# A hybrid attention and SwiGLU layer: own places for each attention unit's stages, four-block products at the end, an opening in pieces over two queues

## The chip, the cores and the metric

One core of a Trainium2 chip runs the whole layer. The metric is device time in microseconds, the median of the runs shown. A run of this kernel varies by some 0.1%.

## The reference

A decoder layer on x (1 x 1024 x 1024, float32). Cut to what matters:

```python
h = rms_norm(x, ln_pre_mix)
proj = h @ w_in                       # pool 256, q 768, k 768, v 768
q, k = rope(q, pos), rope(k, pos)
pool_out = multi_scale_pool(u_pool, w_pool, pool_scale)
attn_out = dilated_attention(q, k, v) # 12 heads of 64; (window, dilation) (128,1) (512,4) (2048,16)
mix = concat([pool_out, attn_out]) @ w_out
x = x + rms_norm(mix, ln_post_mix)
h = rms_norm(x, ln_pre_ffn)
f = (silu(h @ w_gate) * (h @ w_up)) @ w_down
x = x + rms_norm(f, ln_post_ffn)
```

The three attention branches are merged per position and head by their softmax denominators.

## The kernel before, in words

Everything is kept transposed, features on the partitions and the 1024 positions along the free axis, in two halves h of 512. Every float32 operand is split into a high part (a rounded copy, made on ACT) and a low part (the rest, made on DVE or POOL), and a product is three passes on the tensor engine (PE): high x high, high x low, low x high (PASSES). PE's products are issued in program order (`mm`). On the other engines Tile's scheduler orders the instructions by priority, except for those given to `keep_in_program_order`, which keep their order among themselves.

*The opening* (lines 196 to 283). x comes in 8 tiles of 128 x 1024 (512 KB) through `load_x` (L234), the weights of the first head pair, w0[0] for q and w0[1] for k, in columns 0 to 2 and 2 to 8 of their 8 blocks through `load_w` (L226), all on SP's queue. Per x tile ACT makes the high part with g1 as its scale (L239), DVE the low part (L240), ACT a square (L246), DVE the running sum of squares (L248). `first(i, k)` (L220) has the 12 products of 512 columns of tile k for i: 6 for q, 6 for k. Ten products on zeros run ahead of it. The first value weights wv0 are split behind it (L273, with L154 and L158); products for v follow.

*The attention* (lines 304 to 880) has 12 units, one per head pair and half. A unit's stages are: scores (8 steps; PE, then the masked minimum on DVE, L554, and the exponential on ACT, L557), merge (`join`, L567: it exchanges row values through PE with ex, L577, and computes the weights wv in small DVE operations, L583 to L597), weigh (16 steps that scale the probabilities, on DVE, L611, or POOL, L613, by the table 'wd'), turn (transposes on PE, L653, split by ACT, L658, and DVE, L659) and products with v (L685), whose sums pass through L693, L694 and `into` (L623 to L627). Between them stand fill products: the projections of later pairs, of v and of the pool, in lists of 24 or so steps. At the end of a projection half `rope` (L331) runs: shuffle (L320) and cosine product (L321) on DVE, sine product (L322) and sum (L325) by the tables 'rq' and 'rk' on DVE (1) or POOL (0). 'we' says who makes the low part of a weight tile (1: DVE).

The order is a plan written by numbers: `put(steps, lo, hi)` lays a list of steps evenly between two places on an axis on which unit u starts at u, and `emit` (L782) issues all steps sorted by place. The table PRM holds the places: s0 and s1 for the scores, m for the merge, w0 and w1 for weigh, t0 and t1 for the turns, v0 and v1 for the products, one set for units of half 0 ('h0'), one for half 1 ('h1'). Besides, a planner clock runs along with assumed costs: where a step's due time has not come (`await_`, L368; 'lm' for the merge, 'lt' for a turn, 'ls' for a score bank), up to 'fl' fill products are pulled ahead.

*The rest.* The output projection, gate and up products and the down product follow, the latter as seven products of half-size blocks (P1 to P7). P3 is the last; it is cut into columns 0 to 256 and 256 to 512, each with an End (L1371): squares (L1390) and their sum as each row block is ready, the mean on PE (L1404), a power on POOL (L183), a transposition that spreads it (L1412), then `add(d)` for the 8 row blocks: a product with g4 and the spread value on DVE (L1418), the sum with x on DVE or POOL (L1422), and a transfer out (L1426) on SP's or ACT's queue.

Of the kernel before, what the change touches and what calls it, by code (L numbers as in the profile page):

```python
# [15 lines left out]
P = 128  # L16
T = 1024
# [13 lines left out]
        'sqa': (1, 0, 0, 1, 0, 0, 0, 1),  # L31
        'we': (1, 1, 1, 0, 0, 0, 0, 0, 0, 0, 1, 1),
        'nt0': 0.505,
        'nt1': 0.51,
        'oq': (0, 1, 1, 1, 0, 0, 0, 1),
        'lag': 3.0,
        'hp': 150,
        'fl': 12,
        'lt': 3.0,
        'ls': 2.2,  # L40
        'lm': 2.8,
        'lw': (3.5, 0.5),
        'nm': 0.02,
        'n2': -0.07638,
        'n0': 0.14,
        'n1': 0.3,
        'h0': {'s0': 0.0436,
               's1': 0.42346,
               'm': 0.62035,
               'w0': 0.76,  # L50
               'w1': 1.1342,
               't0': 0.85648,
               't1': 1.84986,
               'v0': 1.2506,
               'v1': 1.99965},
        'h1': {'s0': 0.0,
               's1': 0.55,
               'm': 0.63061,
               'w0': 0.76,
               'w1': 1.3742,  # L60
               't0': 0.96118,
               't1': 1.84958,
               'v0': 1.09322,
               'v1': 1.95471,
               'u0': 0.13504,
               'u1': -0.04663,
               'u2': 0.2974,
               'u3': 0.5838},
        'f0': -0.00645,
        'f1': 0.0,  # L70
        'first': {'s0': 0.48, 's1': 0.62, 'm': 0.7, 'w0': 0.78, 'w1': 1.06, 't0': 1.1},

        'vt': ((1.06, 1.08), (2.97, 3.3), (4.97, 5.3), (6.97, 7.3), (8.97, 10.27), (9.83, 10.29)),
        'pw': 0.5,
        'pm': (0.92, (0.78, 0, 0), (0.84, 1, 0), (0.99, 0, 1), (1.05, 1, 1)),
        'last': {'w1': 1.28, 't1': 1.62, 'v1': 1.74},
        'rq': (0, 0),
        'rk': (0, 0),
        'r0': (1, 1),
        'r1': (1, 1),  # L80
        'r2': (1, 1),
        'r3': (1, 1),
        'wd': (0, 1, 1, 0, 0, 0, 0, 0, 0, 0, 1, 0, 0, 0, 0, 0),
        'lr': (10.14, 10.15, 10.26, 10.27),
        'lw0': (10.1, 10.3),
        'lc': (11.63, 11.64, 11.66, 12.1),
        'o0': 10.36,
        'o1': 11.12,
        'o2': 12.85,
        'np': 11.62,  # L90
        'z0': 11.7,
        'z1': 13.05,
        'c0': (0.13, 0.2, 0.21, 0.6, 0.3, 0.7, 0.97, 0.09),
        'c1': (0.16, 0.25, 0.26, 0.84, 0.46, 0.97, 1.57, 1.7),
        'c2': ((0.95, 1.35), (1.4, 1.6)),
        'e0': ((0.26, 0), (0.42, 0), (0.47, 0.9)),
        'e1': (((1.08, 0), (1.28, 0), (1.3, 1.9)), ((2.0, 0), (2.01, 0), (2.02, 2.03)))}
# [10 lines left out]
def hybrid_block(ctx: ExitStack, tc: tile.TileContext, xT, w_in, w_v, w_pin, w_pool, w_out, w_gate, w_up, w_down,  # L108
# [44 lines left out]
    def split(dst, src, eng):  # L153
        nc.scalar.activation(dst[:, 0], src, AF.Copy)  # L154
        n = src.shape[-1]
        w = n if eng is nc.vector else n // 2
        for at in range(0, n, w):
            eng.tensor_tensor(dst[:, 1, at:at + w], src[:, at:at + w], dst[:, 0, at:at + w].bitcast(F32), ALU.subtract)  # L158
# [37 lines left out]
    g1s = cload(g1, [P, NK], "g1s", con1)  # L196

# [6 lines left out]
    nc.scalar.activation(small.tile([P, 1], F32, name="none", tag="none", bufs=1), ones, AF.Copy)  # L204
# [3 lines left out]
    for i in range(10):  # L208
        mm(wb, warm[:, :P], warm, start=True, stop=True)
# [10 lines left out]
    def first(i, k):  # L220
        for a, b in PASSES:
            for h in range(2):
# [3 lines left out]
    def load_w(i, lo, hi):  # L226

        sl = slice(lo * P, hi * P)
        nc.sync.dma_start(w0r[i][:, sl].rearrange("p (k m) -> p k m", m=P), w_in[i][:, lo:hi])
        split(w0[i][:, :, sl], w0r[i][:, sl], nc.vector)  # L230
# [3 lines left out]
    def load_x(k, lo=0, hi=T):  # L234
        if lo == 0:
            xr0.append(att.tile([P, T], F32, name="xraw", tag="pp", bufs=PPB))
        r, sl = xr0[k], slice(lo, hi)
        nc.sync.dma_start(r[:, sl], xT[:, k, sl])
        nc.scalar.activation(xk[k][:, 0, sl], r[:, sl], AF.Copy, scale=g1s[:, k:k + 1])  # L239
        nc.vector.scalar_tensor_tensor(xk[k][:, 1, sl], r[:, sl], g1s[:, k:k + 1], xk[k][:, 0, sl].bitcast(F32),  # L240
                                       op0=ALU.mult, op1=ALU.subtract)

    def square(k):
        r = xr0[k]
        d = att.tile([P, T], F32, name="jk", tag="ptr", bufs=PTB) if k else sq
        nc.scalar.activation(d, r, AF.Square)  # L246
        if k:
            nc.vector.tensor_tensor(sq, sq, d, ALU.add)  # L248

    load_x(0, 0, 512)  # L250
    load_w(0, 0, 2)
    load_x(0, 512, T)
    load_w(1, 0, 2)
    for i in range(2):
        first(i, 0)
    load_x(1)
    for i in range(2):
        load_w(i, 2, NK)
    for i in range(2):
        first(i, 1)  # L260
    for k in range(2, NK):
        load_x(k)
        square(k - 2)
        if k < NK - 2:
            for i in range(2):
                first(i, k)
# [36 lines left out]

    def pinned(x):
        return tc.keep_in_program_order(x)
# [404 lines left out]
    def pool_weights():  # L710
        for n in range(2):
            pool.w[n] = wtile(w_pin[n], nc.vector)

    def pool_proj(tt, k, n):

        if k == n == 0 and tt % 2 == 0:
            pool.ps = bank("t" if tt % 4 else "pj")
        ps = pool.ps[:, (tt % 2) * 256:(tt % 2) * 256 + 256]
        a, b = PASSES[n]
        mm(ps, xk[k][:, b, tt * P:(tt + 1) * P], pool.w[k // 4][:, a, (k % 4) * 256:(k % 4) * 256 + 256],  # L720
           start=(k + n == 0), stop=(k == NK - 1 and n == 2))
        if k == NK - 1 and n == 2 and tt % 2:
            h = tt // 4
            if tt % 4 == 1:
# [7 lines left out]
            due["u", h] = clock[0] + 3.2  # L732

# [7 lines left out]
    def pool_means(i, h):  # L741

        did(("means", i, h))
        await_(("u", h))
# [128 lines left out]
    fill[10] += [vl[12:]]  # L873
    for u in range(1, 11):
        put(Fill([x for f in fill[u] for x in f]).by(3), u + (G["f0"] if u > 1 else -0.07), u + (0.25 if u == 10 else 1) + G["f1"])
# [3 lines left out]
    put([pool_bands], G["pw"], 0)  # L879
# [491 lines left out]
    class End:  # L1371


        def __init__(self, h):
            self.h, self.jk, self.x, self.n = h, {}, [], 0

        def load(self):
            for n in range(2):
                x = place(("b4", "b5")[n], [P, 4, 512], F32, "xe")
                nc.sync.dma_start(x, x1d[4 * n:4 * n + 4, :, self.h * 512:self.h * 512 + 512].rearrange("k p t -> p k t"))  # L1380
                self.x += [x[:, i] for i in range(4)]

        def add(self, d, lo, hi, last):
# [4 lines left out]
            else:  # L1388
                jk = strip("p", 2)[:, :hi - lo]
                nc.scalar.activation(jk, src, AF.Square)  # L1390
                if last:
                    self.jk[lo] = jk
                else:
                    nc.vector.tensor_tensor(self.sq[:, lo:hi], self.sq[:, lo:hi], jk, ALU.add)
            self.n += 1

        def finish(self, lo, hi, tags):
# [17 lines left out]
            def add(d):  # L1415
                yd = yrow(self.h, d)[:, lo:hi]
                at_end = self.h and hi == 512
                i = nc.vector.scalar_tensor_tensor(yd, yd, g4s[:, d:d + 1], box["rb"], op0=ALU.mult, op1=ALU.mult)  # L1418
                eng = nc.gpsimd if at_end and d in (0, 2, 4) else nc.vector
                if at_end:  # L1420
                    tc.keep_in_program_order(i)
                i = eng.tensor_tensor(yd, yd, self.x[d][:, lo:hi], ALU.add)  # L1422
                if at_end and eng is nc.vector:
                    tc.keep_in_program_order(i)
                at = self.h * 512
                (nc.scalar if hi == 512 and self.h and G["oq"][d] else nc.sync).dma_start(  # L1426
                    out[d * P:(d + 1) * P, at + lo:at + hi], yd)
            return [mean], [rows], [lambda d=d: add(d) for d in range(NK)]
# [142 lines left out]
```

## Time and profile before

| | |
|---|---|
| median of 3 runs | 1167.78 us (1166.33 to 1168.17) |
| the profiled execution's own time | 1168.91 us |
| its span (first to last instruction) | 1167.1 us |
| mean granted PE clock | 0.990 |
| PE, DVE, POOL, ACT busy | 97%, 68%, 52%, 47% |
| instructions | 17255 |
| moved by DMA | 188.51 MB |

The profile is one execution. A stage is judged by what PE waits for in it, since PE carries the work: the groups, the waits and the windows are read for the stage, and not for the whole span.

### The profile page before, as it was taken

Reading aid. Unit: us, or ns where it says so; the run is one execution under the profiler, and the core shown is the slowest. Engines: PE = TensorE matmul, PEld = TensorE weight load, DVE = VectorE, ACT = ScalarE, POOL = GpSimd, SP = SyncE. Lnnn points to the kernel's source line nnn. Section 1 sums busy time; section 2 is a strip of 40 time slices with the busy share of each in tenths; the row PEclk is TensorE's granted clock in tenths of the full one; section 3 lists DMA queues with packets and bytes.
Section 4 is the critical chain, followed back from the end, with each engine's and each line's share of the span. In section 5 each row is a group of like instructions: output and inputs, shape, how many; then the busy total and the mean of one; then the engine's idle time right before and its main releaser. Section 6 shows DMA issues by size and latency. Waiting matters only on the chain.

```text
span 1167.1 us, 17255 instructions
## 1 busy us (share of the span) xinstructions
PE 1136.1 (97%) x6134; PEld 980.1 (84%) x6134; DVE 791.6 (68%) x1477; ACT 543.1 (47%) x1033; POOL 608.9 (52%) x541
## 2 busy tenths in 40 slices
PE   8999999999998999999999999999999999999996
PEld 6998889989888888888888888888888888888896
DVE  7766778787887675779686665766565465454685
ACT  7356667666566575656433222232232435343420
POOL 0111546565555403160586667777675978656521
PEclk9999999999999999999999999999999999999998
DMA  7315151415124744732233545444535789666542
GB/s 271 102 60 181 37 181 37 159 59 181 55 73 152 281 162 145 280 118 99 87 143 145 185 155 206 163 171 174 188 139 190 266 292 322 207 210 191 178 144 72
DMA packets 85365, 188.51 MB, mean 162 GB/s; under 512 B 8736, under 2 KB 24352, under 8 KB 83872
## 3 DMA queue, kind: packets, MB, share of 16 engines
q1 hardware_dynamic: 84704, 186.90, 46.2%
q8 instruction: 48, 0.79, 0.3%
q10 hardware_dynamic: 576, 0.52, 0.1%
q14 instruction: 37, 0.30, 0.1%
HBM read 134.44 MB, written 52.95 MB: 161 GB/s over the span
## 4 chain that ended last, share of the span: by engine, by line
PE 80%; DVE 8%; ACT 4%; DMA 3%; issue 3%; POOL 1%; SPq 0%; ACTq 0%; POOLq 0%; DVEq 0%
PE ps_pj L113 28%; PE ps_o L113 22%; PE ps_s L113 20%; PE ps_t L113 8%; PE ps_t L116 2%; ACT pp L557 1%; DMA mixd<-mix 1%; DVE z L1041 1%; DVE z L1040 1%; DMA m<-mixd 1%; DMA b<-in_w_out_dram 1%; DVE k L345 1%; DVE whl L158 1%; ACT whl L154 1%; DMA xraw<-in_xT_dram 1%
## 5 line engine op out<-in xcount | busy, mean ns | idle before, releaser
L113 PE MATMUL ps_pj<-x,whl 128*128 128x512 f32 x480 | 145.9, 418 | 0.0
L1225 POOL TENSOR_TENSOR fw<-rw,fw 128x512 fp32r<-128x512 f32 x74 | 102.6, 1414 | 62.9 <-ACT fw L1223 62.9
L613 POOL TENSOR_SCALAR pp<-pp,wv 128x256 f32<-128x256 f32 (+1 forms) x156 | 72.0, 480 | 104.9 <-DVE wv L597 52.1
L113 PE MATMUL ps_o<-tT,fw 128*128 128x512 f32 x504 | 118.1, 390 | 0.0
L158 POOL TENSOR_TENSOR whl<-wraw,whl 128x512 fp32r<-128x512 f32 x50 | 66.5, 1350 | 90.4 <-ACT whl L154 61.0
L113 PEld LDWEIGHTS ps_o<-tT,fw 128*128 128x128 f32 x504 | 94.6, 188 | 20.3
L557 ACT ACTIVATE pp<-pp,sx 128x128 f32<-128x128 f32 (+1 forms) x192 | 89.3, 468 | 30.0 <-DVE sx L554 29.4
L113 PEld LDWEIGHTS ps_pj<-x,whl 128*128 128x128 f32 x480 | 87.4, 194 | 10.3 <-POOL whl L158 0.4
L1225 POOL TENSOR_TENSOR whl<-rw,whl 128x512 fp32r<-128x512 f32 x42 | 62.5, 1511 | 58.0 <-ACT whl L1223 58.0
L1223 ACT ACTIVATE fw<-rw 128x1024 fp32r<-128x1024 f32 x37 | 38.5, 1058 | 100.7 <-DVE rw L1191 42.4
L113 PE MATMUL ps_pj<-whl,x 128*128 128x256 f32 x528 | 80.3, 293 | 0.0
L1367 POOL TENSOR_TENSOR op<-rw,op 128x512 fp32r<-128x512 f32 x38 | 60.6, 1594 | 35.5 <-ACT op L1366 34.2
L659 DVE TENSOR_TENSOR ptr<-ps_t,ptr 128x512 fp32r<-128x512 f32 (+1 forms) x84 | 56.2, 669 | 26.4 <-ACT ptr L658 25.8
L113 PEld LDWEIGHTS ps_pj<-whl,x 128*128 128x128 f32 x528 | 70.7, 196 | 0.5 <-DVE whl L158 0.2
L322 POOL TENSOR_TENSOR rsw<-rsw,sinr 128x512 f32<-128x512 f32 x20 | 26.2, 1309 | 84.7 <-DVE rsw L320 84.7
L658 ACT ACTIVATE ptr<-ps_t 128x512 fp32r<-128x512 f32 (+1 forms) x84 | 48.4, 576 | 40.6 <-PE ps_t L116 39.4
L1366 ACT ACTIVATE op<-rw 128x1024 fp32r<-128x1024 f32 x38 | 40.2, 1060 | 56.3 <-PE ps_t L113 32.2
L113 PE MATMUL ps_o<-ptr,v 128*128 128x128 f32 (+1 forms) x472 | 58.6, 258 | 4.8 <-DVE ptr L659 4.8
L113 PE MATMUL ps_pj<-b,fw 128*128 128x512 f32 x264 | 62.3, 392 | 0.0
L113 PEld LDWEIGHTS ps_o<-ptr,v 128*128 128x128 f32 x472 | 52.6, 164 | 8.8 <-DVE ptr L659 5.9
L113 PEld LDWEIGHTS ps_pj<-b,fw 128*128 128x128 f32 x264 | 49.6, 188 | 10.9
L113 PE MATMUL ps_s<-k,qh 128*128 128x128 f32 (+1 forms) x192 | 53.6, 291 | 0.3 <-DVE sx L554 0.2
(302 smaller groups left out, 2914.9 us busy)
## 6 DMA issues: line engine op xcount, KB each, us to landing
rw<-bd SPq DMA_DIRECT2D x77, 256.0 KB, 4.5
v<-vd SPq DMA_DIRECT2D x22, 512.0 KB, 4.9
rw<-wsd SPq DMA_DIRECT2D x44, 256.0 KB, 4.0
rw<-in_w_gate_dram SPq DMA_DIRECT2D x20, 512.0 KB, 3.6
rw<-in_w_up_dram SPq DMA_DIRECT2D x20, 512.0 KB, 4.5
bd<-p SPq DMA_DIRECT2D x33, 256.0 KB, 2.9
rw<-in_w_down_dram SPq DMA_DIRECT2D x33, 256.0 KB, 4.4
fw<-in_w_down_dram SPq DMA_DIRECT2D x16, 512.0 KB, 4.1
```

The costliest lines, as they stand in the source:

```text
L113: return tc.keep_in_program_order(nc.tensor.matmul(*a, **k))
L116: return tc.keep_in_program_order(nc.tensor.transpose(dst, src, by))
L158: eng.tensor_tensor(dst[:, 1, at:at + w], src[:, at:at + w], dst[:, 0, at:at + w].bitcast(F32), ALU.subtract)
L322: eng[0].tensor_tensor(s, s, sinr[:, sl], ALU.mult)
L557: nc.scalar.activation(pt[:, j, lo:], pt[:, j, lo:], AF.Exp, bias=sx[:, 0, side, j, hd, 0:1], scale=-1.0, accum_out=sx[:, 0, side, j, hd, ...
L613: nc.gpsimd.tensor_scalar(pv, pv, un.wv[:, side, j, hd:hd + 1], 1.0, op0=ALU.mult, op1=ALU.mult)
L658: nc.scalar.activation(ptr[:, 0, :w], t[:, :w], AF.Copy)
L659: nc.vector.tensor_tensor(ptr[:, 1, :w], t[:, :w], ptr[:, 0, :w].bitcast(F32), ALU.subtract)
L1223: nc.scalar.activation(w[n][:, :, 0], raw[n], AF.Copy)
L1225: low[0] = nc.gpsimd.tensor_tensor(w[n][:, i, 1], raw[n][:, i], w[n][:, i, 0].bitcast(F32), ALU.subtract)
L1366: nc.scalar.activation(w[:, :, 0], raw, AF.Copy)
L1367: nc.gpsimd.tensor_tensor(w[:, 0, 1], raw[:, 0], w[:, 0, 0].bitcast(F32), ALU.subtract)
```

## The change

It has three parts.

1. *Places.* PRM gets other values nearly throughout, and a new table 'du' with offsets of up to 0.08 for the places of single units. Some of the values: 'lm' 2.8 to 3.081, 'lt' 3.0 to 2.819, 'ls' 2.2 to 2.382, 'fl' 12 to 15; 'rk' (0, 0) to (1, 0): the sine product of each K rope goes from POOL to DVE; 'r0' (1, 1) to (0, 1): one sine product of the opening goes to POOL; 'wd' gets a fourth 1 among 16; 'we' from (1,1,1,0,0,0,0,0,0,0,1,1) to (0,0,0,0,0,1,0,0,0,1,1,1); 'pm', the places of the pool means, from (0.84, 1, 0), (0.99, 0, 1), (1.05, 1, 1) to (0.857, 1, 0), (1.025, 0, 1), (1.05, 1, 1), with their products 0.06 behind each. 'cut' is empty and 'pb' is 0, so `dealt` and the place of the bands change nothing.
2. *Opening.* `load_x` and `load_w` become fetch and split; all of them are pinned in program order. g1 and the first weight columns are issued on ACT's queue; x tiles 0 and 1 come and are split in halves of 512 columns, the weights in columns 0 to 2, 2 to 4 and 4 to 8; the squares move behind the splits; the last x tile has a buffer of its own; 8 products on zeros instead of 10.
3. *End.* For half 1 the scaling by g4 moves to ACT, behind each square; the product with the spread value and the sum with x take four or two row blocks at once; four transfers of 256 KB per cut instead of eight of 128 KB.

```diff
@@ the units
         g = dict(G, **G["h1" if h else "h0"])
+        g.update({k: g[k] + d for k, d in G["du"].get(u, {}).items()})
@@ the opening
+    g1s = con1.tile([P, NK], F32, name="g1s")
+    pinned(nc.scalar.dma_start(g1s, g1))
+    fetch_x(0, 0, 512)
     for i in range(2):
-        first(i, 0)
-    load_x(1)
+        fetch_w(i, 0, 2, nc.scalar)
...
+    fetch_x(0, 512, T)
+    fetch_x(1, 0, 512)
+    fetch_x(1, 512, T)
     for i in range(2):
-        load_w(i, 2, NK)
+        fetch_w(i, 2, 4)
+    fetch_x(2)
     for i in range(2):
-        first(i, 1)
+        fetch_w(i, 4, NK)
+    split_x(0, 0, 512)
+    split_w(0, 0, 2)
+    split_w(1, 0, 2)
+    for i in range(2):
+        first(i, 0, (0,))
+    split_x(0, 512, T)
+    for i in range(2):
+        first(i, 0, (1,))
+    for h in range(2):
+        split_x(1, h * 512, h * 512 + 512)
+        if h:
+            for i in range(2):
+                split_w(i, 2, 4)
+        for i in range(2):
+            first(i, 1, (h,))
     for k in range(2, NK):
-        load_x(k)
-        square(k - 2)
+        if k > 2:
+            fetch_x(k)
+        split_x(k)
+        if k == 2:
+            for i in range(2):
+                split_w(i, 4, NK)
+        for d in range(*((0, 1), (1, 1), (1, 2), (2, 3), (3, 4), (4, 6))[k - 2]):
+            square(d)
         if k < NK - 2:
             for i in range(2):
                 first(i, k)
@@ End
+            if self.h:
+                nc.scalar.activation(src, src, AF.Copy, scale=g4s[:, d:d + 1])
...
+            def times(n):
+                yd = yblock("%d2" % (n + 1))[:, :, lo:hi]
+                pin(nc.vector.tensor_tensor(yd, yd, box["rb"][:, None].to_broadcast([P, 4, hi - lo]), ALU.mult))
+
+            def plus(n, i, eng, queue, each):
+                yd, xd = yblock("%d2" % (n + 1))[:, i:i + 2, lo:hi], self.x4[n][:, i:i + 2, lo:hi]
+                for k in range(0, 2, each):
+                    o = eng.tensor_tensor(yd[:, k:k + each], yd[:, k:k + each], xd[:, k:k + each], ALU.add)
+                    if eng is nc.vector:
+                        pin(o)
+                at = (4 * n + i) * P
+                queue.dma_start(out[at:at + 2 * P, 512 + lo:512 + hi].rearrange("(d p) t -> p d t", p=P), yd)
+
+            sums = ((1, 0, nc.gpsimd, nc.scalar, 1), (1, 2, nc.vector, nc.sync, 2), (0, 0, nc.vector, nc.scalar, 2),
+                    (0, 2, nc.vector, nc.sync, 2))
+            if hi < 512:
+                sums = [(n, i, nc.vector, nc.sync, 2) for n, i, *_ in sums]
```

More of the change, by code (lines that the diff above doesn't have):

```diff
@@ L56 @@
[L56 to L71, printed above, removed]
@@ new lines @@
+ 'we': (0, 0, 0, 0, 0, 1, 0, 0, 0, 1, 1, 1),
+ 'nt0': 0.505,
+ 'nt1': 0.51,
+ 'lag': 3.0,
+ 'hp': 150,
+ 'fl': 15,
+ 'lt': 2.819,
+ 'ls': 2.382,
+ 'lm': 3.081,
+ 'lw': (3.551, 0.5),
+ 'nm': 0.02,
+ 'n2': -0.10991,
+ 'n0': 0.14241,
+ 'n1': 0.29735,
+ 'h0': {'s0': 0.02145,
+        's1': 0.42346,
+        'm': 0.62035,
+        'w0': 0.77676,
+        'w1': 1.1342,
+        't0': 0.85648,
+        't1': 1.83344,
+        'v0': 1.2506,
+        'v1': 1.99965},
+ 'h1': {'s0': 0.0,
+        's1': 0.55,
+        'm': 0.63061,
+        'w0': 0.76,
+        'w1': 1.36042,
+        't0': 0.97415,
+        't1': 1.84958,
+        'v0': 1.09414,
+        'v1': 1.95471,
+        'u0': 0.13504,
+        'u1': -0.04663,
+        'u2': 0.32076,
+        'u3': 0.61876},
@@ L98 @@
+ 'f0': -5e-05,
+ 'f1': 0.0,
+ 'first': {'s0': 0.4784, 's1': 0.61071, 'm': 0.68269, 'w0': 0.77241, 'w1': 1.06, 't0': 1.1},
+ 'vt': ((1.08276, 1.10953),
+        (2.97, 3.3),
+        (4.98923, 5.40466),
+        (6.97, 7.30064),
+        (8.78313, 10.27869),
+        (9.8514, 10.28666)),
+ 'pw': 0.5,
+ 'pb': 0.0,
+ 'pe': 1,
+ 'cut': {},
[47 rows of a table added]
 ON_DVE = ((0, 1),)
@@ L207, in hybrid_block @@
     wb = bank("o")
-    for i in range(10):
+    for i in range(8):
         mm(wb, warm[:, :P], warm, start=True, stop=True)
@@ L873, in hybrid_block, with dealt @@
     fill[10] += [vl[12:]]
+    def dealt(lists, cut):
+        if cut is None:
+            return [x for f in lists for x in f]
+        n, back, ahead = cut
+        a, b = lists[n], lists[n + 1]
+        lists = lists[:n] + [a[:len(a) - back], b[:ahead], a[len(a) - back:], b[ahead:]] + lists[n + 2:]
+        return [x for f in lists for x in f]
     for u in range(1, 11):
[L875 removed]
+        put(Fill(dealt(fill[u], G["cut"].get(u))).by(3), u + (G["f0"] if u > 1 else -0.07), u + (0.25 if u == 10 else 1) + G["f1"])
     both = {}
@@ L1425, in add @@
[L1425 to L1428, printed above, removed]
+                nc.vector.scalar_tensor_tensor(yd, yd, g4s[:, d:d + 1], box["rb"], op0=ALU.mult, op1=ALU.mult)
+                nc.vector.tensor_tensor(yd, yd, self.x[d][:, lo:hi], ALU.add)
+                nc.sync.dma_start(out[d * P:(d + 1) * P, lo:hi], yd)
@@ L1430, in hybrid_block @@
+            if not self.h:
+                return [mean], [rows], [lambda d=d: add(d) for d in range(NK)]
+            sums = ((1, 0, nc.gpsimd, nc.scalar, 1), (1, 2, nc.vector, nc.sync, 2), (0, 0, nc.vector, nc.scalar, 2),
+                    (0, 2, nc.vector, nc.sync, 2))
+            if hi < 512:
+                sums = [(n, i, nc.vector, nc.sync, 2) for n, i, *_ in sums]
+            return [mean], [rows], [lambda n=n: times(n) for n in (1, 0)] + [lambda a=a: plus(*a) for a in sums]
     ends = [End(h) for h in range(2)]
```

116 lines of the change are left out of this document (31 added, 85 removed), and 47 rows, old and new, of the table PRM.

## The prediction

> **What bounds the kernel now.** I read the head of the page first, then the busy time stage by stage, then what the tensor engine (PE) waited for, and last the single stalls and the two ends.
>
> ```profile
> span 1167.1 us, 17255 instructions
> PE 1136.1 (97%) x6134; PEld 980.1 (84%) x6134; DVE 791.6 (68%) x1477; ACT 543.1 (47%) x1033; POOL 608.9 (52%) x541
> ```
> ```profile
> 0.00:15.70 15.70, 11.90 (x37) 7.87 (x37) 8.27 (x13) 11.11 (x15) 2.26 (x8) 1.00 0.82 301
> 60.00:440.00 380.00, 364.14 (x2454) 334.85 (x2453) 289.11 (x847) 238.78 (x637) 174.46 (x229) 0.98 0.37 124
> 440.00:1120.00 680.00, 679.68 (x3057) 560.60 (x3056) 429.75 (x502) 266.04 (x341) 422.09 (x296) 1.00 0.53 185
> 1154.40:1167.10 12.70, 1.65 (x11) 1.08 (x9) 6.68 (x15) 0.42 (x1) 2.86 (x4) 0.60 0.24 83
> ```
>
> PE is busy 97% of the span, and the change removes none of its products, so only idle PE can be won: 31.0 us in all. The second fence (PE, PEld, DVE, ACT, POOL, clock, DMA) places it: 3.8 us in the opening, 15.9 in the attention, 0.3 in the 680 us of gate, up and down products, 11.1 behind the last product. The change can touch the first, second and fourth.
>
> ```profile
> PE ps_o L113 <- DVE ptr L659: 4.8, 4, 1.5
> PE ps_s L113 <- DVE ex L577: 4.4, 3, 2.5
> PE ps_t L116 <- POOL pp L613: 3.0, 2, 2.7
> PE ps_pj L113 <- DMA m<-mixd: 2.2, 2, 1.6
> PE ps_o L113 <- DVE mix L627: 1.0, 1, 1.0
> ```
> ```profile
> 122.65:126.05 3.40, 3.40 (x11) 2.69 (x10) 3.22 (x10) 1.98 (x4) 0.36 (x1) 0.50 0.00 0
> 306.98:310.38 3.40, 3.40 (x13) 2.83 (x12) 2.87 (x8) 1.67 (x3) 1.09 (x1) 0.50 0.48 154
> 344.54:347.93 3.39, 3.39 (x10) 2.72 (x9) 2.28 (x6) 1.33 (x3) 3.39 (x8) 0.50 0.45 158
> 375.26:378.65 3.39, 3.39 (x18) 3.39 (x18) 2.22 (x4) 2.58 (x4) 3.39 (x7) 0.50 0.77 223
> ```
>
> These are the attention's stalls (12 waits, 15.4 us) and four stretches whose granted clock is 0.50. Each takes 3.4 us for 1.7 us of work, so the attention loses 6.8 us more that counts as busy.
>
> ```profile
> 305.84 0.43 PE L113 MATMUL ps_s<-ex,ls 128*128 128x64 f32 x2 [2.51 <-DVE ex L577]
> 342.81 0.62 PE L113 MATMUL ps_o<-ptr,v 128*64 128x256 f32 x5 [1.39 <-DVE ptr L659]
> 343.73 0.44 PE L116 MATMUL ps_t<-idt,pp 128*128 128x128 f32 x2 [0.31 <-POOL pp L613]
> 151.19 0.79 PE L113 MATMUL ps_o<-ptr,v 128*64 128x128 f32 x7 [1.52 <-DVE ptr L659]
> ```
>
> Two halved stretches begin some 1 us behind the stalls at 303 and 341 to 344. The 1.52 us stall at 149.7 to 151.2 has none behind it; the stretches lie 54, 11 and 9 multiples of 3.41 us apart, so I take it that activity is weighed on a fixed grid of 3.41 us, and that about 1.5 us idle inside one step halves the next. A stall that crosses that mark costs 1.7 us on top. The Trainium skill, page "TensorE: Matmul & The Clock Gate", section "HAM oscillation — how this bites in real kernels", has another threshold, "no PE-idle gaps >~3.4µs". By that rule none of these stalls would halve the clock, and the 1.7 us counted below for unit 7 would go; the trace speaks against it with 0.50 behind idle times of 1.7 and 2.5 us.
>
> **The opening.** Same bytes, same products; the x tiles 0 and 1 and the first weights come in smaller pieces, and squares move behind the splits.
>
> ```profile
> 3.05 6.01 DMA xraw<-in_xT_dram
> 14.34 1.29 DVE x L240
> 15.68 1.19 PE ps_s L113 x4
> 16.87 1.37 PE ps_t L113 x6
> ```
> ```profile
> L240 DVE SCALAR_TENSOR_TENSOR x<-xraw,g1s,x 128x1024 fp32r<-128x1024 f32 x7 | 8.9, 1279 | 1.6 <-ACT x L239 1.6
> L248 DVE TENSOR_TENSOR sq<-sq,jk 128x1024 f32<-128x1024 f32 x7 | 8.5, 1217 | 0.0
> L239 ACT ACTIVATE x<-xraw,g1s 128x1024 fp32r<-128x1024 f32 x7 | 7.9, 1141 | 0.9 <-DMA xraw<-in_xT_dram 0.9
> L246 ACT ACTIVATE jk<-xraw 128x1024 f32<-128x1024 f32 x7 | 7.3, 1047 | 1.3 <-DVE sq L248 1.3
> ```
> ```profile
> 9.00:11.00 2.00, 1.82 (x7) 0.86 (x5) 0.73 (x1) 1.92 (x2) 0.00 (x0) 1.00 1.03 412
> ```
>
> In the chain x tile 1 lands at 9.06; the low part of tile 2 is ready at 15.63, and from 15.68 PE runs dry no more: 70 of 96 products are left at 0.228 us (1.37 for 6), to about 31.6. I assume the bytes come no faster: DMA share is already 0.82 up to 15.7 us, two queues or one. Behind tile 1 only 256 KB of weights now stand ahead of the 512 KB of tile 2; at 412 GB/s it lands near 11.0. Its splits then take 1.14 on ACT and 1.28 on DVE: ready near 13.5. ACT next has two weight splits (about 0.6 each, between its rows) and the first square (1.05), so tile 3's ACT split runs 14.4 to 15.55 and its low part is ready near 16.85, where PE has 58 products left: 16.85 + 13.2 = 30.1. That gains 1.5 us. DVE gives some back: behind 16.85 it still has four splits (1.28), seven sums and the split of the first value weights (1.22 each), 14.9 us to 31.7, and PE wants the low part of those weights from about 30.5. Placed last they cost 1.2 us, placed ahead of the last sums nothing; nothing pins them, so I count 0.3. I take **-1.2**; the ends are -2.2 (tile 3 never late: 13.45 + 70 x 0.228 = 29.4) and 0 (the two waits near 12 to 13.5 fall into one 3.41 us step, clock halved once, 1.7). The two warm-up products fewer cost nothing: data are ready before 6 us, and the later halves bound.
>
> **The end.**
>
> ```profile
> 1158.02 0.88 DVE y L1418 x2
> 1158.92 0.66 DVE y L1422
> 1163.86 0.42 DVE y L1422
> ```
> ```profile
> L1418 DVE SCALAR_TENSOR_TENSOR y<-y,g4s,ps_pj 128x256 f32<-128x256 f32 x8 | 3.5, 471 | 1.6 <-PE ps_pj L116 1.6
> 1158.58 0.72 POOL L1422 TENSOR_TENSOR y<-y,xe 128x256 f32<-128x256 f32 x1 [1.34 <-DVE y L1418]
> DMA to landing us min/median/max: 1.7/1.8/1.8
> 1160.00:1161.00 1.00, 0.00 (x0) 0.00 (x0) 0.97 (x3) 0.00 (x0) 0.72 (x1) 0.50 0.75 260
> ```
>
> Before, DVE works alone from 1158.02 to 1164.28: 8 products (0.47) and 5 sums, with POOL on three. After: two products of 1024 columns (1.2 each, as L248's 1024 columns), then three sums of 512 (0.65 from the row 0.42 for 256, plus some 0.25 per 256), beside POOL's two of 0.72. A sum that runs beside POOL takes 0.66 instead of 0.42, so 0.3 is added once: 2.4 + 1.95 + 0.3 = 4.65 against 6.26, a gain of 1.6. The last transfer is 256 KB instead of 128: at the 260 GB/s of the first burst 0.5 longer than the 1.7 of the row. **-1.1**, between -1.8 and -0.6. The g4 scaling goes to ACT behind each square; ACT works 0.42 us in the last 12.7, so it lies beside PE's mean and POOL's power. The four-block form for the lower columns (5 us instead of 7 on DVE) lies under products.
>
> **The attention.** Sorting the steps by their new places gives PE's order; I count the products between producer and consumer, at 0.23 us. At the stalls little opens: scores to merge, unit 7: 4.4 us and 4.4; unit 1: 3.7 and 3.4; unit 9: 3.1 and 2.6. Turn to product, unit 1: 3.3 and 2.6 at the fourth; unit 3: 3.3 and 3.1; unit 7's last: 2.7 and 2.8. First turn behind the merge, unit 9: 5.3 and 5.65. What is moved between engines weighs more: the sine product of every K rope goes from POOL to DVE, one more weighing of 16 to DVE, the split of three weights changes sides.
>
> ```profile
> 337.10 1.28 POOL L322 TENSOR_TENSOR rsw<-rsw,sinr 128x512 f32<-128x512 f32 x1 [5.40 <-DVE rsw L320]
> 340.84 1.28 POOL L325 TENSOR_TENSOR rcl<-rco,rsw 128x512 f32<-128x512 f32 x1
> 340.96 1.19 DVE L594 TENSOR_TENSOR nm<-de 128x16 f32<-128x16 f32 x1
> L590 DVE TENSOR_TENSOR dd<-nm,sx x12: 176/192/1225, 76.1 to 433.5; 128x32 f32<-128x32 f32 x12
> L577 DVE TENSOR_TENSOR ex<-sx,qdA x12: 206/216/1001, 73.1 to 428.1; 128x64 f32<-128x64 f32 x12
> ```
>
> - Around 341: POOL does a K rope's sine (1.28), a weight split and the rope's sum in a row to 342.1. DVE operations of 0.19 (the row L590: least, median, most) take 1.2 beside it. Without the sine POOL is done 1.3 earlier; the product's and turn's stalls (1.39 + 0.31) and the halved clock (1.7) go, less 0.68 for the sine on DVE: -2.7.
> - Unit 7's merge: ex took 1.00 (the most of its row) beside POOL's sine, else 0.22: -0.75, not enough to save the clock.
> - Pool means (1, 1) go ahead of product (0, 1), which keeps their bank from the slow mix: -1.0.
> - Unit 9's first turn: -0.35. The narrowed places (units 9, 1, 1, 3, 1: 0.5 + 0.7 + 0.1 + 0.2 + 0.2): +1.6.
>
> Sum **-3.2**. Not shown by the trace is how DVE's queue orders itself under 6.8 us more of K-rope sines (ten halves at 0.68): at best half of the 22.2 us (15.4 + 6.8) goes, -11; at worst three new halvings, as below, +10.
>
> **Sum.** 1168.9 (profiled execution, 1.8 around its span) - 1.2 - 1.1 - 3.2 = 1163.4. It was 1.1 above the median of 1167.8, so 1162.3, rounded **1162**.
>
> **Rivals.** (1) *Stalls and halvings go together*: a few tenths less at each of four stalls saves the stall and 1.7. For it: idle times of 1.4 to 1.7 lie right at the mark. Against: the distances. With two more stretches saved (2 x 1.7, plus their stalls of some 4): 1155. (2) *Only the ends move*, the stalls wander to other places: 1167.8 - 2.3 = 1165.5; and if DVE also gives back the opening, 1166.7, which is no change. (3) *DVE becomes the bound*, slower: after the change unit 8's merge stands right behind the last product of a K half (24 of 24 against 21), as unit 7's does, and unit 1's just behind a Q half. Shuffle, cosine and now sine (0.75 + 0.68 + 0.68) then precede ex on DVE. It decides where ex comes over 1.5 us late inside one step: 1.8 + 1.7 each, three times: 1162 + 10.5 = 1172.5. For it: DVE is busy 289 of 380 us. Against: ex has high priority.
>
> The Trainium skill, page "DMA: Bandwidth & Descriptors", section "Issuing engines are not separate DMA queues", says that queues of several issuers share the same DMA engines and save only issue time; by that a faster arrival is not to be had, and the opening's -2.2 would be out of reach through the second queue.
>
> **Chances.** Forecast (1158 to 1165) 0.52, rival 1 0.25, rival 2 0.13, rival 3 0.10. The bound of 0.2% (about what a measurement of this kernel tells from no change) is 2.3 us: 1165.4 to 1170.1. Rival 2 lies at its edge and in it; I split its chance. Faster 0.82, within 0.08, slower 0.10. The range of 8 in 10 reaches from below rival 1 to no change: 1153.5 to 1167.5.
>
> **What would show it.** Opening: PE without a wait from about 16.9, its first 96 products done near 30; wrong if it waits for the value weights. End: DVE two products near 1.2 and three sums near 0.65 behind the last transposition, the last sum some 4.6 behind it. Attention: PE's waits for pp L613 and mix gone, fewer than four stretches at 0.50; wrong if ex or ptr waits grow.

## The result, and the profile after

The changed kernel takes 1153.94 us (median of 4 runs, 1153.06 to 1155.68), the kernel before 1167.05 beside it (4 runs, 1165.22 to 1168.17): a ratio of 0.9891, 95% interval 0.9872 to 0.9909. The gain is 13.1 us where 5.8 was forecast. The profiled execution took 1154.33. One execution says little about a few us: 19 of the kernel before, beside kernels 1 to 4, took 1164.26 to 1170.04.

The head of the page after, then the same stages by windows (columns: stretch, its length, busy PE, PEld, DVE, ACT, POOL, granted clock, DMA share, GB/s):

```profile
span 1152.5 us, 17226 instructions
PE 1129.9 (98%) x6132; PEld 977.3 (85%) x6132; DVE 792.7 (69%) x1484; ACT 553.0 (48%) x1048; POOL 591.7 (51%) x517
```
```profile
0.00:15.70 15.70, 13.79 (x47) 10.03 (x48) 9.60 (x16) 11.81 (x18) 2.27 (x8) 1.00 0.90 331
60.00:440.00 380.00, 372.29 (x2557) 344.28 (x2556) 302.12 (x882) 249.50 (x652) 158.48 (x213) 1.00 0.38 130
440.00:1120.00 680.00, 678.23 (x3060) 560.43 (x3060) 431.45 (x508) 264.93 (x339) 421.79 (x289) 1.00 0.53 185
1140.50:1152.50 12.00, 1.54 (x11) 0.99 (x9) 5.10 (x7) 0.93 (x2) 2.11 (x3) 0.63 0.26 87
```

In the attention PE is idle 7.7 us instead of 15.9. The same PE instructions in both traces, counted from the span's start, say where the time went:

```
PE reaches                        before    after   gained so far
the first product for v            31.68    28.69    3.0
the spread of the row factors      39.94    40.18   -0.2
the first attention scores         56.87    56.38    0.5
the merge of unit 4               211.36   206.22    5.1
the merge of unit 7               302.95   295.33    7.6
the merge of unit 10              398.62   383.34   15.3
the last product with v           458.87   443.19   15.7
the last product of all          1154.41  1140.53   13.9
the end of the span              1167.09  1152.55   14.5
```

So the opening gave 0.5 to the first scores, the attention 15.2, the end 0.7; 1.8 was lost between, most of it in one wait of 1.26 us for the second norm's power at 457. PE's waits from 60 to 440 us (total, times, longest), after:

```profile
PE ps_t L146 <- POOL pp L669: 3.7, 3, 3.0
PE ps_s L143 <- DVE ex L633: 1.6, 1, 1.6
PE ps_o L143 <- DVE ptr L715: 1.3, 3, 0.6
```

With four smaller groups it is 7.6 us, against 15.8 before with its smaller ones. The wait for the split of the transposed probabilities (ptr) fell from 4.8 to 1.3, that for ex from 4.4 to 1.6, those for mix are gone. Of stretches at half clock the attention keeps one of four, and the opening has a new one:

```profile
34.18:37.58 3.40, 3.40 (x18) 3.40 (x18) 3.40 (x6) 0.00 (x0) 0.79 (x1) 0.50 0.76 199
365.30:368.70 3.40, 3.40 (x18) 3.40 (x18) 3.31 (x8) 0.63 (x2) 3.40 (x7) 0.50 1.03 419
```

8.2 us of waits and three stretches of 1.7 make 13.3 of the attention's 15.2; the rest is in pieces that the list of waits does not show. The number of stretches belongs to these two executions: one stretch is worth 0.0015 of the mean granted clock, and over the same 19 executions of the kernel before that clock goes from 0.990, the value of its profile, to 0.994. The two traces lie 14.5 us apart, the medians 13.1.

### The profile page after: what moved, and what is told of

Same layout as the page of the kernel before. It is cut to its first block, busy times and chain, and to the rows that moved or that the text cites. A ratio compares the mean times of both kernels' runs of the same rounds, so it can differ in the third digit from the quotient of the medians.

```text
span 1152.5 us, 17226 instructions
## 1 busy us (share of the span) xinstructions
PE 1129.9 (98%) x6132; PEld 977.3 (85%) x6132; DVE 792.7 (69%) x1484; ACT 553.0 (48%) x1048; POOL 591.7 (51%) x517
## 5 line engine op out<-in xcount | busy, mean ns | idle before, releaser
L143 PE MATMUL ps_pj<-x,whl 128*128 128x512 f32 x480 | 142.0, 409 | 0.0
L143 PE MATMUL ps_s<-k,ql 128*128 128x128 f32 (+1 forms) x192 | 52.9, 284 | 0.0
```

The lines of the kernel that those rows point to most:

```text
L143: return tc.keep_in_program_order(nc.tensor.matmul(*a, **k))
```

## The experiments

Two theories at first: the gain of the attention comes from the tables that move work between engines ('rk' above all), or from the places with their unit offsets 'du'. Medians are of their own runs; ratios are to the kernel before.

**The three parts alone.** Kernel 1 is the changed one with the opening and the end of before. Kernels 2 and 3 are the kernel before with the new opening alone and with the new end alone.

> The changed table of places and engines alone, with the opening and the end of before. Theory A (the attention's gain of about 15 us comes from the table, and opening and end have little to do with it): 1153.9 + 0.5 for the opening + 0.7 for the end, 1155 us. Theory B (the new opening shifts the queues of DVE and ACT so that the attention's stalls fall elsewhere): most of the 15 us is missing, about 1165 us.

> The new opening alone in the kernel before. Theory A: the first 96 products end 3 us earlier, but a wait for the sum of squares and a half-clock stretch behind it take most of it back, so 1166.5 us, within 0.2% of before. Theory B (opening carries the attention): 1155 to 1160 us.

> The four-block end alone in the kernel before. By the two profiles the end is 0.7 us shorter: 1166.4 us. If the predicted 1.1 us were right: 1166.0. Both lie within 0.2% of before; the profile's time behind the last product tells them apart (12.7 us before, 12.0 with the change).

Places alone: 1155.97, ratio 0.9903 (0.9888 to 0.9918), as theory A had it. Opening alone: 1171.59, 1.0040 (1.0025 to 1.0055), slower, which neither theory expected. End alone: 1165.54, 0.9991 (0.9982 to 1.0001), with 11.7 us behind the last product (12.7 before). Nearly all the gain is in the table of numbers. The new opening alone starts the products for v 2.9 us earlier (28.76) and reaches the first scores 1.25 later (58.12). PE in that kernel, with the idle time and its releaser in brackets, and two stretches:

```profile
31.22 2.36 PE L113 MATMUL ps_o<-ones,sq 128*128 128x1 f32 x16 [0.87 <-DVE sq L253]
```
```profile
32.60:36.00 3.40, 3.40 (x18) 3.40 (x18) 3.40 (x10) 0.18 (x1) 1.66 (x1) 0.50 0.56 154
107.70:111.10 3.40, 3.40 (x13) 3.06 (x13) 1.47 (x5) 0.55 (x2) 0.00 (x0) 0.50 0.96 313
```

PE waits for the sum of squares and, from the 16 one-column products on, runs 6.8 us at half clock (32.6 to 39.4; the first row shows half of it). The second row is one of three such stretches in the attention, where the trace before has four, and the waits there add up to 15.9 us against 15.8. So between the two traces all of the loss, 1.3 us of span, is there at the first scores. The medians lie 5.0 apart; where the other 3.7 come from no trace shows.

**The tables.** Kernel 4 is the kernel before with the new 'we', 'wd', 'rk' and 'r0' at the old places; kernel 5 the changed kernel with these four as before; kernel 6 the changed kernel with 'rk' alone as before:

```diff
- 'rk': (1, 0),
+ 'rk': (0, 0),
```

> Only the engine tables of the change (K ropes' sine on DVE, one more weighing on DVE, three weight splits on the other side, one opening sine on POOL) in the kernel before, at the old places. Theory A1 (the tables carry the attention's gain, by taking POOL off the shared work): 1155 to 1158 us. Theory A2 (the places carry it): 1166 us or more, since DVE gets some 11 us of work more at places that were not made for it.

> The changed kernel with the engine tables of before (K ropes' sine back on POOL, weighing and weight splits as before), places kept. The tables alone in the kernel before brought nothing (1166.7). Theory P (the places alone carry the gain): 1154 us, within 0.3% of the changed kernel. Theory PT (places and tables carry it together: DVE's queue has to be empty of POOL-blocked work where a split is due): some half of the 12 us comes back, 1158 to 1162 us, with waits for ptr or pp above 1 us in the units.

> The changed kernel with only the K ropes' sine back on POOL ('rk' as before). If that move is what frees POOL and with it DVE: some stalls with POOL-blocked K splits come back, 1157 to 1160 us. If any engine will do at these places: 1154 us.

At the old places the tables bring nothing: 1166.70, 0.9998 (0.9986 to 1.0010). There too PE's wait for ptr falls, from 4.8 us to 1.3, but others come in its place (pp 6.1 instead of 3.0, sx 1.6 instead of 0.2), and the sum is 15.3 us instead of 15.8. In the changed kernel their loss costs 6.8 (1160.73; 0.9946, 0.9928 to 0.9964), and 'rk' alone 6.2 (1160.17; 0.9953, 0.9938 to 0.9968). The waits of kernel 6, in a profiled execution of 1164.20 that is the slowest of its six:

```profile
PE ps_o L46 <- DVE ptr L618: 4.5, 4, 1.9
PE ps_t L49 <- POOL pp L572: 3.0, 1, 3.0
PE ps_s L46 <- DVE ex L536: 2.6, 2, 2.3
```

With K's sine back on POOL, PE waits for ptr nearly as before (4.5; 4.8 before, 1.3 after), and for ex in part (2.6; 4.4 and 1.6). So the move of that sine carries what was won on ptr and some of ex. At the old places the tables take the ptr waits away as well; only at the new ones does nothing else come in their place.

**Without the offsets.** Kernel 7 is the changed kernel with an empty 'du'; in kernel 8 'du' holds units 3 and 5 only.

> The changed kernel without the per-unit offsets ('du' empty), all else kept. Theory U (each unit's own offset of up to 0.08 matters, since one operation of 1.3 us ahead of a split makes a stall): 1158 to 1163 us. Theory G (the common places and tables carry the gain): 1153 to 1156 us.

> The changed kernel with the offsets of units 3 and 5 alone; those of the ten others are taken out. Without any offsets the profile has two waits of 4.7 us for weighed rows, at the first turns of units 3 and 5, each with a half-clock stretch behind it: 12.8 us. Theory Q (the offsets work by the order of single large operations in a queue, here a value-weight split of 2.5 us ahead of POOL's weighing): both waits go, 1171.4 - 12.8 = 1158.6, 1157 to 1160 us. Theory S (the offsets act by distances, a little in each unit): the waits shrink in part, 1163 to 1168 us.

Without offsets: 1171.39, ratio 1.0040 (1.0025 to 1.0055), 17.5 us above the changed kernel, for numbers of at most 0.08; both theories expected 1163 at most. PE in it, and the half clock behind its second stall:

```profile
190.82 1.32 PE L49 MATMUL ps_t<-idt,pp 128*128 128x128 f32 x4 [4.66 <-POOL pp L572]
```
```profile
254.70:258.10 3.40, 3.39 (x11) 2.61 (x12) 2.10 (x4) 0.60 (x1) 3.40 (x8) 0.50 0.66 222
```

Two waits of 4.66, at the first turns of units 3 and 5, make 9.3 of the 17.5. The half clock behind them, 6.8 us long at the first (189.8 to 196.7, its first 1.0 still in the wait) and 3.4 at the second, makes another 4.6. With the offsets of these two units alone both waits stay (1171.49; 1.0035, 1.0024 to 1.0046): theories Q and S both fell. What VectorE and GpSimd did ahead of the first stall (start, duration, engine, line):

```profile
186.25 0.72 DVE L279 STREAM_SHUFFLE rsw<-ps_pj 128x512 f32<-128x512 f32 x1
...
187.38 2.49 POOL L91 TENSOR_TENSOR whl<-wraw,whl 128x512 fp32r<-128x512 f32 x2 [5.02 <-ACT whl L87]
187.46 1.22 DVE L556 TENSOR_TENSOR wv<-nm,dd 128x16 f32<-128x16 f32 x1
...
189.84 1.89 POOL L572 TENSOR_SCALAR pp<-pp,wv 128x256 f32<-128x256 f32 x3
```

The weights wv are the last small operation of the merge. A rope's shuffle and its cosine product stand ahead of it on VectorE; then it runs into GpSimd's weight split and takes 1.22 us instead of 0.17, and the weighing stands behind that split. In the changed kernel the order in the same unit is the other way round:

```profile
181.46 0.17 DVE L653 TENSOR_TENSOR wv<-nm,dd 128x16 f32<-128x16 f32 x1
...
181.80 4.35 POOL L669 TENSOR_SCALAR pp<-pp,wv 128x256 f32<-128x256 f32 x9 [3.56 <-ACT low L749]
...
183.91 0.73 DVE L376 STREAM_SHUFFLE rsw<-ps_pj 128x512 f32<-128x512 f32 x1
```

Kernel 9 has no offsets either, and makes the low parts of the two value weights in question, (n, h) = (1, 1) and (2, 0), on VectorE, so that GpSimd is free:

```diff
-box["w"] = [wv0 if n + kk == 0 else wtile(w_v[n][kk]) for kk in range(2)]
+box["w"] = [wv0 if n + kk == 0 else wtile(w_v[n][kk], nc.vector if (n, h) in ((1, 1), (2, 0)) else None) for kk in range(2)]
```

> No offsets at all, but the four value-weight tiles that were split on POOL behind the merges of units 3 and 5 (second half of the second, first half of the third group) are split on DVE. Theory Q: POOL is free when the weights wv are ready; the two waits of 4.7 us shrink to 2 us or less and their half-clock stretches go, 1171.4 to about 1162 (5 us of work more on DVE may bring others). Theory S: the waits stay near 4.7 us, 1171 us.

1172.74 (1.0044, 1.0029 to 1.0059): each wait becomes two of 2.2, for GpSimd's and VectorE's weighings. That is theory S's time and not theory Q's: GpSimd's split is not the cause by itself; the weights are late (184.18 where the wait had begun at 182.87).

**Order or place.** What was left was the order on VectorE (theory O) or the places of PE's products (rival P). The offsets of single units decide the order in units far from them: with those of unit 2 alone wv stands ahead of the rope in unit 3 only, with those of unit 6 alone in unit 5 only, without those of unit 2 in unit 5 only. The last of the four kernels has no offsets at all; PE's instructions are in the same order, row for row, as in kernel 7, and two instructions are given to `keep_in_program_order`:

```diff
-        nc.vector.stream_shuffle(s, ps, SWAP16)
+        pinned(nc.vector.stream_shuffle(s, ps, SWAP16))
...
-        nc.vector.tensor_tensor(wv.rearrange("p s j a -> p (s j a)"), nm, dd[:, 0], ALU.mult)
+        pinned(nc.vector.tensor_tensor(wv.rearrange("p s j a -> p (s j a)"), nm, dd[:, 0], ALU.mult))
```

> The changed kernel with the unit offsets left for unit 2 alone; all the other offsets are away. What is open: without any offsets two waits of 4.66 us stand at the first turns of units 3 and 5, and with the offsets of units 3 and 5 alone both stay. Theory O: the wait is not set by where PE's turn stands but by VectorE's order: where the shuffle of a rope (L279) stands ahead of the value weights wv (L556), the weights come 3 us or more too late, because the rope's operations run beside GpSimd's split and take over 1 us each. In the order of this kernel wv stands ahead of that rope in unit 3 and behind it in unit 5. So theory O expects the wait in unit 3 gone (under 1.5 us), the wait in unit 5 of about 4.6 us left, and a time about 6 us (one wait and one half-clock stretch of 1.7 us) under 1171.4, some 1165. Rival P: the offsets matter by the places of the units' own products on PE; unit 2's offsets are not those of unit 3, so both waits stay and the time is 1171.

> The changed kernel with the unit offsets left for unit 6 alone. The mirror of the run with unit 2: here VectorE's order has wv ahead of the rope in unit 5 and behind it in unit 3. Theory O expects the wait in unit 5 gone (under 1.5 us), the wait in unit 3 of about 4.6 us left, some 1165. Rival P (places of a unit's own products on PE): both waits stay, 1171.

> The changed kernel with all unit offsets but those of unit 2. VectorE's order has the rope ahead of wv in unit 3 again, and wv first in unit 5. Theory O expects one wait of about 4.6 us at the first turn of unit 3 and none in unit 5: 1154 + 4.7 + 1.7 = 1160, within 2 us. Rival P: no wait comes back (the offsets of unit 3 are still there), 1154.

> The changed kernel without any unit offsets, in which VectorE's shuffle of each rope and the value weights wv are held in the order in which the program writes them. PE's order of instructions is the same, row for row, as in the kernel without offsets; VectorE has wv ahead of the rope in units 3 and 5. Theory O: both waits go (under 1.5 us each) and with them two half-clock stretches: 1171.4 - 2*(4.66 + 1.7) = 1158.7, within 3 us. Rival P: PE's order sets the waits, so they stay and the time is 1171. Rival R: the weights come earlier, but the rope then comes late and PE waits for its product's bank or for the rotated rows: 1163 to 1171, with a wait for ps pj or qh in their place.

PE's waits for the weighing on GpSimd between 180 and 255 us in these kernels, unit 2 alone first, then unit 6 alone, all but unit 2, weights first (total, times, longest):

```profile
PE ps_t L49 <- POOL pp L572: 5.4, 2, 4.7
```
```profile
PE ps_t L49 <- POOL pp L572: 5.9, 2, 4.6
```
```profile
PE ps_t L49 <- POOL pp L572: 4.9, 2, 4.6
```
```profile
PE ps_t L49 <- POOL pp L572: 3.0, 2, 1.5
```

In the first three one long wait is left, in the unit where the rope stands first: unit 5, unit 3, unit 3. In the other unit it is 0.78 + 0.73, 1.25 + 1.18 and 0.34. In the fourth both are 1.5. The times: 1166.71 (0.9998, 0.9985 to 1.0010), 1169.37 (1.0020, 1.0010 to 1.0031), 1159.87 (0.9937, 0.9917 to 0.9958) and 1162.31 (0.9958, 0.9943 to 0.9973). The waits are where theory O put them in all four, and rival P is out: the fourth kernel has kernel 7's order on PE and is 9.1 us faster. The sizes fit less well: the unit 6 kernel came 4 us above the expected time, and its remaining wait of 2.4 above the expected 1.5. The fourth came 3.6 above its 1158.7, outside the 3 allowed, and 8.4 above the changed kernel; it has another wait of 1.44 for the weighing, in unit 1, and what else the offsets give stays open. Rival R's waits, for ps_pj or qh, are not in its trace. In the fourth kernel the weights come at 186.03 and the weighing on GpSimd at once:

```profile
186.03 0.17 DVE L556 TENSOR_TENSOR wv<-nm,dd 128x16 f32<-128x16 f32 x1
...
186.37 2.02 POOL L572 TENSOR_SCALAR pp<-pp,wv 128x256 f32<-128x256 f32 x4 [4.03 <-DVE wv L556]
```

The kernel before had no such stall in units 3 and 5. So the offsets did not win 17 us over it; they take away two stalls that the change's other numbers bring in.

**The opening's pieces.** Kernel 10 has 'nm' (the place of the products that sum the squares) at 0.04 instead of 0.02; in kernel 11 the first weights are fetched on SP's queue like all else.

```diff
-        fetch_w(i, 0, 2, nc.scalar)
+        fetch_w(i, 0, 2)
```

> The changed kernel with the mean of squares behind 18 instead of 12 value products ('nm' 0.02 to 0.04), one edit. Theory H (the 0.76 us wait for the sum of squares sets off the half-clock stretch at 34.2): wait and stretch go, 2.4 us, 1151.5 us, less what a later chain of norms costs. Rival (the 16 one-column products count as idle and halve the clock whatever precedes them): the stretch stays, 1153 us.

> The changed kernel with the first weight columns on SP's queue again, in the same pieces and order. If the second queue brought the bytes earlier, x tile 1 lands later than 6.9 us and the first 96 products end later than 28.7 us by 0.5 or more; if the pieces alone did it, both stay. The time of the whole changes by less than 0.1%, 1153 to 1155 us, since the wait for the sum of squares takes what is won.

'nm' 0.04: 1152.80 (0.9882, 0.9865 to 0.9898). Its profiled execution is the slowest of four (1156.10 at a clock of 0.991; the others 1151.79 to 1153.38 at 0.993 to 0.995). In it a wait of 0.59 for the sum of squares stays and so does the halved stretch, so this kernel does not tell theory H from its rival. Other traces speak against both as they stand: in the kernel before the same 16 products run at 33.12 without a wait, in kernel 3 at 33.46, and the clock stays at 1.00; kernel 9 waits 0.90 there and keeps it too. One queue: 1156.58 (0.9901, 0.9884 to 0.9917), above the expected 1153 to 1155; its trace has four half-clock stretches where that of the changed kernel has two. The two halves of x tile 1 landed at 7.13 and 7.79 us there, at 6.22 and 6.90 with two queues, and the whole tile at 9.06 before; the products for v start at 29.43 instead of 28.69.

**A faster version.** Kernel 12 is the changed kernel with 'nm' at 0.08 and the low part of the last value weights (tiles == (2,)) made on VectorE, against the wait of 3.0 that is left in unit 9.

> The changed kernel with two edits that act 330 us apart: the mean of squares behind 30 value products ('nm' 0.08), and the last value weights split on DVE. Theory Q: the remaining 3.0 us wait at unit 9's first turn has a value-weight split of 2.5 us ahead of the weighing on POOL; on DVE it costs 1.2, so the wait shrinks to 1 to 1.5 us and its half-clock stretch goes: -3 us. At the opening the wait goes (0.8 us); the stretch behind it goes if the wait set it off. Together 1149 to 1150 us; 1152 where the stretch at 33 us stays.

1151.48 (1151.14 to 1151.99); 0.9865 (0.9851 to 0.9880), below both kernels, but above the expected 1149 to 1150. The opening gave 1.3 of the 2.3 us between the two spans: the stretch around the sum of squares keeps its clock, and the first scores come at 55.07 instead of 56.38. The rest lies for the most part (0.9) behind the last product with v; its cause stays open.

```profile
32.70:36.10 3.40, 3.40 (x29) 3.40 (x30) 3.40 (x6) 0.01 (x1) 1.08 (x1) 1.00 0.34 87
```

The wait in unit 9 only shrank to 2.6 and 0.3, and its half-clock stretch stayed (362.9). In the changed kernel's trace it is the same order again: a shuffle at 357.13 ahead of the merge's last operations, of which three then take 0.91, 1.19 and 0.90 beside GpSimd.

## Why the prediction was right in direction and wrong in size

The time lies in the range, 0.4 us above its lower end, but the gain is over twice the forecast. The mis-sized term is the attention: -3.2 forecast, -15.2 measured.

- **Opening, -1.2; measured -0.5.** The first step failed on the good side: "I assume the bytes come no faster" does not hold, with tile 1 at 6.90 instead of 9.06, and PE runs without a wait from 8.39 on, not from 16.9. The products for v start 3.0 earlier, past the forecast's end of 2.2. Kernel 11 puts 0.9 of the tile's 2.2 on the second queue; that leaves the rest to the pieces and the order of the fetches. What the forecast did not have is what is late next: PE meets the sum of squares.

```profile
28.69 1.48 PE L143 MATMUL ps_pj<-k,x 128*128 128x256 f32 x11
...
31.05 1.95 PE L143 MATMUL ps_o<-ones,sq 128*128 128x1 f32 x16 [0.76 <-DVE sq L283]
```

  It waits 0.76 there, and the halved stretch from 34.18 takes 1.7 more. The forecast watched the value weights' split; the wait came two steps later on the same VectorE queue. The Trainium skill, page "DMA: Bandwidth & Descriptors", section "Issuing engines are not separate DMA queues", says that a second issuing engine saves only issue time, which is usually small beside the transfer. The traces agree on what is saved: SP issues the tile's second half at 2.12 us instead of 3.08 and it lands 0.9 earlier, in an opening whose whole gain is of that size.

- **End, -1.1; measured -0.7.** The arithmetic of VectorE was right, the transfer was mis-sized.

```profile
1143.96 2.35 DVE L1495 TENSOR_TENSOR y<-y,ps_pj 128x1024 f32<-128x1024 f32 x2 [1.44 <-PE ps_pj L146]
1145.31 1.41 POOL L1500 TENSOR_TENSOR y<-y,xe 128x256 f32<-128x256 f32 x2 [2.01 <-issue]
1146.22 2.25 DVE L1500 TENSOR_TENSOR y<-y,xe 128x512 f32<-128x512 f32 x3
```
```profile
DMA to landing us min/median/max: 2.2/2.5/2.7
```

  Two products of 1.2 and three sums of 0.75 end at 1148.47, 4.5 us behind the start of the first where 4.65 was forecast and 6.26 stood before. But the span ends 4.1 us behind the last sum, where it was 2.8: a transfer of 256 KB lands 2.2 to 2.7 us behind its issue instead of 1.7 to 1.8, and the last ones share 335 to 349 GB/s.

- **Around 341, -2.7; measured -3.0.** Right: 1.39 + 0.31 and the halving became 0.38.
- **Unit 7's merge, -0.75, "not enough to save the clock".** The wait went from 2.51 to 1.55, and the halving went as well: -2.7. The second half of that is luck of the execution: the traces of kernels 10 and 11 have the same wait, 1.52, and a half-clock stretch right behind it (299.62 and 300.13).
- **Pool means, -1.0.** The wait for mix of 0.95 became one for dhl of 0.34. The waits for the mix rows from memory (2.2) went too; that was not forecast, and it is not all the change's: kernel 3, with the attention of before, has 0.6.
- **Unit 9's first turn, -0.35.** Wrong by sign: 2.70 became 3.00, with its halving.
- **The narrowed places, +1.6** (its parts add up to 1.7). This is the step that failed. It counted the products between a producer and its consumer on PE and took the producer's side, the order of VectorE's queue and the time of its operations, as it was. The four waits at those places in units 1 and 3 (1.48, 0.42, 1.52, 1.45) vanished, -4.9, and so did the halving at 122, another 1.7; that one hangs on the execution, for kernels 2 and 3 keep the wait of 1.48 without it. The distance did shrink (unit 1, from the last score product to the first of the merge, 3.40 us to 2.79). At 1.48 and 1.52 the order changed. Before, a rope's shuffle and cosine product stood ahead of ex, and Q's low parts ahead of ptr:

```profile
119.52 0.73 DVE L320 STREAM_SHUFFLE rsw<-ps_pj 128x512 f32<-128x512 f32 x1
...
120.74 0.99 DVE L577 TENSOR_TENSOR ex<-sx,qdA 128x64 f32<-128x64 f32 x1
```
```profile
149.01 1.40 DVE L352 TENSOR_TENSOR ql<-rco,qh 64x512 fp32r<-64x512 f32 x2
150.44 0.69 DVE L659 TENSOR_TENSOR ptr<-ps_t,ptr 128x512 fp32r<-128x512 f32 x1
```

  After, ex starts at 117.14 and the shuffle at 117.62, and ptr stands ahead of Q's parts:

```profile
142.62 0.68 DVE L715 TENSOR_TENSOR ptr<-ps_t,ptr 128x512 fp32r<-128x512 f32 x1
...
144.47 0.86 DVE L407 CAST qh<-rco 64x512 fp32r<-64x512 f32 x2
```

  At 0.42 and 1.45 the producers' time changed. The row before and after of the low parts of K behind a rope, and the last of the four places in the trace before:

```profile
L345 DVE TENSOR_TENSOR k<-rcl,k 64x512 fp32r<-64x512 f32 x20 | 17.1, 855 | 0.6
```
```profile
L401 DVE TENSOR_TENSOR k<-rcl,k 64x512 fp32r<-64x512 f32 x20 | 15.2, 758 | 3.6 <-ACT k L400 2.9
```
```profile
202.54 3.00 POOL L158 TENSOR_TENSOR whl<-wraw,whl 128x512 fp32r<-128x512 f32 x2
...
203.44 2.65 DVE L345 TENSOR_TENSOR k<-rcl,k 64x512 fp32r<-64x512 f32 x2
...
206.12 0.69 DVE L659 TENSOR_TENSOR ptr<-ps_t,ptr 128x512 fp32r<-128x512 f32 x1
```

  Before, GpSimd does the rope's sine and comes to its weight split at 202.5, so that the two low parts run beside it and take 2.65 instead of 1.4; ptr, queued behind them, starts at 206.12, 2.4 us behind its input from ACT, and PE waits 1.45. After, the sine is on VectorE and the same two take 1.41, from 192.62 on, with GpSimd idle. Kernel 6, with the sine back, has the two ptr waits of unit 1 back (1.13 and 0.99, with Q's low parts ahead of ptr again); in unit 3 the two low parts take 3.00 again, and PE waits 1.35 there, for scores that stand behind them on VectorE. So at these three places the sine is the cause. The ex wait of unit 1 is not back; which of the new places removed it is not shown. For the longer times beside GpSimd the Trainium skill has a mechanism, page "SBUF — State Buffer", section "Who interferes with whom": a VectorE instruction with two inputs in SBUF contends with a GpSimd instruction that reads SBUF, and the ports they share are an exclusive lock. The row of wv at 187.46 agrees: it ends at 188.68, when the first half of the split that began at 187.38 (2.49 for two) ends, near 188.6.
- **"Not shown by the trace is how DVE's queue orders itself"** was named as the open end, -11 to +10. That is where the result lay, 4 us beyond the better end. Rival 1 (stalls and halvings go together, 1155) comes nearest. Rival 3 (VectorE becomes the bound, 1172.5) is near what the same change does without its offsets, 1171.4, and by the mechanism that was named, a shuffle and a cosine product ahead of the merge, only at wv and not at ex.

Left open: why the new opening alone ends 5.0 us above the kernel before by the medians, and the 1.9 us of the attention's gain that no row shows.

## What to carry to other kernels

Between engines that work through queues in order, ask of each small operation at a stall what stands ahead of it in its queue and what GpSimd runs beside it, before counting the distance on the busy engine. A change of a planner's numbers moves that order far from the place it names (the offsets of unit 2 decide a 4.6 us wait in unit 3), so read the order of the compiled queues; where one order matters, pin it. Look at what is late next when an opening gets faster: here 3.0 us were won and 3.2 lost again within twelve.

## What the runs showed of the hardware

- Half clock around the sum of squares goes, in these traces, with the wait and the 16 one-column products together. Take steps of 3.41 us, counted from each trace's own half-clock stretches, and add up in each step PE's idle time and the time of these products. In ten of the 18 traces a step reaches 1.97 us or more (0.28 + 1.95 in the changed kernel), and a stretch at 0.50 begins right behind it; in the other eight no step comes above 1.84 (1.04 before, 0.54 + 1.01 in kernel 12), and none begins. Few busy columns seem to weigh like idle time; no run varied that alone. The Trainium skill, page "TensorE: Matmul & The Clock Gate", section "HAM oscillation — how this bites in real kernels", asks only for no idle gaps over about 3.4 us; the row of 0.50 from 34.18, behind a wait of 0.76, speaks against that as a safe bound.
- VectorE operations of 0.16 to 0.19 us took 0.9 to 1.2 beside GpSimd's sine, split and sum, three within one merge in unit 9.
